# Decoding a candidate's position in a top-k router: sums of comparisons in place of shifts, casts and predicated copies

## The chip, the cores and the metric

The kernel runs on one core of one Trainium2 chip. The metric is the device time of one launch in microseconds (us), lower is better. Three runs of the kernel before gave a median of 3564.58 us (3550.21 to 3570.75).

## The reference

One layer of a hybrid decoder over 1024 tokens of width 1024: a token mixer with three parallel branches (stick-breaking attention, native sparse attention, a gated linear recurrence), merged by sigmoid gates, and then a feed-forward block of experts that are found by product keys. The change lies in that last block, which for a chunk of 128 tokens is

```python
qh = (xc @ w_q).reshape(Ct, 8, 2, 64)
s = jnp.einsum("nhad,akd->nhak", qh, sub_keys)            # 128 sub-keys per half
top_s, top_i = lax.top_k(s, 16)                           # 16 best of each half
cand = (top_s[:, :, 0, :, None] + top_s[:, :, 1, None, :]).reshape(Ct, 8, 256)
cand_idx = (top_i[:, :, 0, :, None] * 128 + top_i[:, :, 1, None, :]).reshape(Ct, 8, 256)
best_s, pos = lax.top_k(cand, 16)
eidx = jnp.take_along_axis(cand_idx, pos, axis=-1)        # one of 16384 experts
gate = jax.nn.softmax(best_s, axis=-1)
hpre = jnp.einsum("nd,nhkd->nhk", xc, u_tab[eidx])
act = gate * gelu(hpre)
y = jnp.einsum("nhk,nhkd->nd", act, v_tab[eidx])
```

So each token has 8 heads and 16 experts per head. From a position in the list of candidates the router has to recover the two ranks, a (in the first half's list) and b (in the second's), and from these the two sub-key numbers.

## The kernel before

**Tiles and parts.** The 1024 tokens are eight tiles of 128 tokens, in four parts of two tiles. The mixer, the merge, the scores and the route of each part are emitted one after the other. The expert block is computed in two ways. For parts 1 and 2 (tiles 2 to 5, 512 tokens) it is dense: a loop over 128 expert groups of 128 experts multiplies all 512 tokens with every expert, and gates that are zero for experts not chosen (kept in DRAM as d_G, loaded as `gt`) do the selection. For parts 0 and 3 (tiles 0, 1, 6 and 7) the rows of u and v are gathered: per tile 128 indirect DMAs for u and 128 for v, issued by GpSimd, each followed by one VectorE update of 128x1024 (`gather_tile`: L1147 for u, L1157 for v into `gacc`). These gathers and updates run beside other work: those of tiles 0 and 1 beside the later parts' mixer, those of tiles 6 and 7 beside the dense loop. Their landing rows cycle through five buffers (eleven for part 3, some of them named `rr_u` and `rr_v`). The tile's index list (`gidx`) has a single buffer and is read by all of its 256 gathers.

**The route of a tile.** `route` (L985) builds for each head 72 candidates instead of 256, since a pair of ranks a and b can be among the 16 best only if (a+1)(b+1) is at most 16. They lie in four blocks: positions 0 to 31 are 2 ranks a by 16 ranks b, 32 to 47 are 2 by 8, 48 to 63 are 4 by 4, 64 to 71 are 8 by 1. The position of a chosen candidate, `p2` (128x128: 8 heads of 16), is decoded to a and b (L1034 to L1048). Then the ranks become one-hot masks of 128x2048 (`oneh`, L1060), which are multiplied with the sub-key numbers (`tir`, put there by ScalarE) and summed by halving (L1064, L1065). For gathered tiles `routes` makes the expert number (L1177), casts it to `idx` (L1178) and stores it; GpSimd's gathers of the tile load it from there. For dense tiles `keep_route` and `spread_pieces` turn ranks and gates into d_G (`hot` on VectorE, `gb` on TensorE).

**Who sets the order.** Two layers. First a plan in Python: pieces of VectorE and TensorE work are emitted by a model of both engines' load; `account` adds up 0.06 us plus elements/960 per VectorE instruction, and a piece is emitted when an engine's load lies below what is due. A route is a generator, and each of its steps up to a `yield` is such a piece; ROUTE_STEPS says how many there are per tile. The pieces of the last part's tail (merge, scores, routes of tiles 6 and 7) go to the list `ending`; those that are left when the dense loop starts are emitted in the loop, TP = 3 behind each expert group. The 1024 gather updates are spread over the plan's steps by `paced`. Then a scheduler orders each engine's instructions by a simulated timeline, so the built order is not the one written.

**The shared ring.** Eight buffers of 128x512 with the tag "at" (`W2` with its defaults) are handed out in turn: to fa, fb and ua of a route (the fields that the decode works in), to its candidate lists and `tir`, to the gelu outputs `ge` of the dense loop and to a copy of a PSUM bank there. A new tenant waits until the one before it in that buffer has been read for the last time.

**The dense loop.** Group i+3's first matmul (`g`, L258) runs ahead of group i's second one (into six PSUM accumulators `acc` and one in SBUF, L1436, L1445). ScalarE makes `ge` from `g` (L1395), VectorE multiplies with `gt` (L1429), and every f32 operand is split into two f16 halves, the high by ScalarE (L213) and the low by VectorE (L214): `us`, `vs` and `ac`.

Of the kernel before, what the change touches and what calls it, by code (L numbers as in the profile page):

```python
# [71 lines left out]
def trunk(ctx: ExitStack, tc: tile.TileContext, a: dict, out: bass.AP):  # L72
# [921 lines left out]
    def route(pt, tile_no, ts_, ti_, gate):  # L994
# [36 lines left out]
        V.tensor_tensor(gate, mb, gz.unsqueeze(2).to_broadcast([128, 8, 16]), op=ALU.mult)  # L1031
        yield

        V.tensor_copy(pf, p2)  # L1034

        V.tensor_scalar(t_u, p2, 4, None, op0=ALU.logical_shift_right)
        V.tensor_copy(af, t_u)
        V.tensor_scalar(t_u, p2, 15, None, op0=ALU.bitwise_and)
        V.tensor_copy(bf, t_u)

        for start, sh, sub, mask in ((32, 3, -2.0, 7), (48, 2, -8.0, 3), (64, 0, -56.0, 0)):
            V.tensor_scalar(t_m, pf, float(start) - 0.5, None, op0=ALU.is_gt)
            V.tensor_scalar(t_u, p2, sh, None, op0=ALU.logical_shift_right)
            V.tensor_scalar(t_f, t_u, sub, None, op0=ALU.add)
            V.copy_predicated(af, t_m, t_f)
            V.tensor_scalar(t_u, p2, mask, None, op0=ALU.bitwise_and)
            V.tensor_copy(t_f, t_u)
            V.copy_predicated(bf, t_m, t_f)  # L1048
            yield

        shape = [128, 16, 16, 8]
        tif = SM(f"tif_{nm}", [128, 8, 2, 16], F16, bufs=1)
# [1 line left out]
        for x, sel in ((0, af), (1, bf)):  # L1054
            tir = W2(f"tir{x}_{nm}", (128, 8, 16, 8), F16)
            S.activation(tir, tif[:, :, x, :].unsqueeze(3).to_broadcast([128, 8, 16, 8]), AF.Copy)
            selh = SM(f"selh{x}_{nm}", [128, 16, 8], F16, bufs=1)
            V.tensor_copy(selh, sel.rearrange("p (g w) -> p g w", w=8))
            oh_ = WT(f"oneh{x}_{nm}", pt, x, shape, F16)
            V.tensor_tensor(oh_, selh.unsqueeze(2).to_broadcast(shape), iota16r.unsqueeze(1).to_broadcast(shape), op=ALU.is_equal)  # L1060
            o4 = oh_.rearrange("p (h u) b w -> p h u (b w)", u=2)
            V.tensor_tensor(o4, o4, tir.rearrange("p h b w -> p h (b w)").unsqueeze(2).to_broadcast([128, 8, 2, 128]), op=ALU.mult)
            for w in (8, 4, 2):
                V.tensor_tensor(oh_[:, :, 0:w, :], oh_[:, :, 0:w, :], oh_[:, :, w:2 * w, :], op=ALU.add)  # L1064
            V.tensor_tensor(sel.rearrange("p (g w) -> p g w", w=8), oh_[:, :, 0, :], oh_[:, :, 1, :], op=ALU.add)  # L1065
            yield
# [97 lines left out]

    found = {}

    ROUTE_STEPS = 11

    def routes(pt, tl, tsa, tia):

# [394 lines left out]
```

## Time and profile before

| what | before |
|---|---|
| median of three runs | 3564.58 us (3550.21 to 3570.75) |
| the profiled execution | 3556.94 us |
| its span | 3555.1 us, mean granted TensorE clock 0.937 |
| TensorE (PE) busy | 3255.7 us, 92% |
| VectorE (DVE) busy | 3001.0 us, 84%, 6662 instructions |
| ScalarE (ACT) busy | 1599.9 us, 45% |
| GpSimd (POOL) busy | 1360.4 us, 38% |
| DRAM traffic | 944.19 MB read, 110.10 MB written, 297 GB/s |

How to read it: one execution is recorded by the hardware profiler. Times are us unless marked ns. L12 is line 12 of the kernel. In a row "out<-in" are the names of the tiles, without their running numbers; fa_rt, fb_rt and ua_rt are the three fields of a route, so the decode's rows carry those names. The bracket at the end of a row of a timeline gives the time that the engine stood idle before the instruction, and what ended it. PE is TensorE, PEld its loading of weights, DVE VectorE, ACT ScalarE, POOL GpSimd. A busy share over the whole span is a mean over stages with different limits. An engine that idles and isn't the limit of a stage costs nothing there.

### The profile page before, as it was taken

How to read it: one execution, taken by the hardware profiler on the slowest of the kernel's cores; microseconds unless marked ns; L12 is line 12 of the kernel's file. 1: busy time of each engine (PE TensorE's matmuls, PEld its weight loads, DVE VectorE, ACT ScalarE, POOL GpSimd, SP SyncE). 2: the span in 40 equal slices, each digit the busy share in tenths (PEclk: the TensorE clock that was granted, in tenths of full speed). 3: DMA queues.
4: the chain of work that ended last, by engine and by line, in shares of the span. 5: the costliest groups of instructions: out<-in, count | busy, mean ns of one | idle time of the engine just before them, and what ended most of it. 6: DMA issues, size and time to landing. Idle time of an engine off the chain costs nothing.

```text
span 3555.1 us, 57087 instructions
## 1 busy us (share of the span) xinstructions
PE 3255.7 (92%) x20660; PEld 2181.6 (61%) x20660; DVE 3001.0 (84%) x6662; ACT 1599.9 (45%) x3162; POOL 1360.4 (38%) x1166
## 2 busy tenths in 40 slices
PE   7999899999997799999878879869999999999996
PEld 6887777777876587887666644434444444444443
DVE  5665669888789888888998868999988998989898
ACT  5776454653543465644356333234334333333332
POOL 0000001343332242223322234347764765766664
PEclk9999999999997799999778899989999999999998
DMA  8964865989977587897656799789998999999997
GB/s 303 322 240 150 279 206 197 327 314 311 360 284 239 170 307 253 307 331 277 219 190 214 278 353 332 242 267 372 388 375 314 375 381 351 371 352 380 342 373 260
DMA packets 359336, 1058.07 MB, mean 298 GB/s; under 512 B 35238, under 2 KB 107626, under 8 KB 354444
## 3 DMA queue, kind: packets, MB, share of 16 engines
q0 software_dynamic: 147456, 536.94, 42.1%
q1 hardware_dynamic: 206988, 483.93, 38.4%
q10 hardware_dynamic: 4608, 33.56, 2.4%
q8 instruction: 162, 2.65, 0.3%
q14 instruction: 122, 1.00, 0.1%
HBM read 944.19 MB, written 110.10 MB: 297 GB/s over the span
## 4 chain that ended last, share of the span: by engine, by line
PE 53%; DVE 23%; DMA 9%; issue 7%; ACT 6%; POOL 1%; SPq 0%; ACTq 0%; DVEq 0%; POOLq 0%
PE g L258 13%; PE acc L1436 10%; PE pj_mg L258 4%; DVE u L1147 4%; PE g L1436 3%; DVE gacc L1157 3%; PE pj_r_hg L258 2%; DMA v<-in_peer_v_dram,gidx 2%; PE pb L258 2%; DMA gt<-d_G 2%; DMA u<-in_peer_u_dram,gidx 2%; PE pj_wo L258 2%; PE gb L1219 1%; PE gb L1220 1%; PE z_sb L410 1%
## 5 line engine op out<-in xcount | busy, mean ns | idle before, releaser
L1155 POOL DMA_INDIRECT v<-in_peer_v_dram,gidx x421 | 553.6, 1315 | 689.8 <-DVE gacc L1157 410.1
L1145 POOL DMA_INDIRECT u<-in_peer_u_dram,gidx x417 | 523.5, 1255 | 636.8 <-DVE u L1147 404.9
L258 PE MATMUL g<-h,us 128*128 128x512 f16 x3072 | 690.8, 382 | 17.1 <-DVE ts L982 6.2
L1157 DVE SCALAR_TENSOR_TENSOR gacc<-v,act,gacc 128x1024 f32<-128x1024 f32 x421 | 538.1, 1278 | 35.4 <-DMA v<-in_peer_v_dram,gidx 31.8
L1436 PE MATMUL acc<-vs,ac 128*128 128x512 f16 x2304 | 536.8, 381 | 20.6 <-ACT vs L213 7.8
L1436 PEld LDWEIGHTS <-ac 128*128 128x128 f16 x3072 | 302.0, 98 | 411.4 <-issue 50.1
L258 PEld LDWEIGHTS <-us 128*128 128x128 f16 x3072 | 302.0, 98 | 385.1 <-issue 17.8
L1147 DVE SCALAR_TENSOR_TENSOR u<-u,gh 128x1024 f32<-128x1024 f32 x417 | 501.8, 1216 | 34.3 <-DMA u<-in_peer_u_dram,gidx 33.8
L1395 ACT ACTIVATE ge<-g 128x512 f32<-128x512 f32 x128 | 76.2, 595 | 528.7 <-PE g L258 498.4
L258 PE MATMUL pj_mg<-hT,w_mg 128*128 128x256 f16 x2304 | 273.9, 274 | 6.3 <-ACT mg L881 3.9
L258 PEld LDWEIGHTS <-w_mg 128*128 128x128 f16 x2304 | 226.8, 100 | 37.6 <-issue 11.8
L1436 PE MATMUL g<-vs,ac 128*128 128x512 f16 x768 | 184.0, 383 | 23.6 <-ACT ge L1395 23.6
L214 DVE SCALAR_TENSOR_TENSOR vs<-vraw,vs 128x1024 f16<-128x1024 f32 x128 | 154.8, 1215 | 25.9 <-ACT vs L213 25.8
L1145 POOL DMA_INDIRECT rr_u<-in_peer_u_dram,gidx x95 | 137.1, 1444 | 89.5 <-DVE rr_u L1147 66.3
L213 ACT ACTIVATE vs<-vraw 128x1024 f16<-128x1024 f32 x128 | 132.6, 1046 | 84.8 <-DMA vraw<-in_peer_v_dram 84.8
L213 ACT ACTIVATE ac<-ge 128x512 f16<-128x512 f32 x128 | 80.0, 628 | 200.7 <-DVE ge L1429 161.3
L1155 POOL DMA_INDIRECT rr_v<-in_peer_v_dram,gidx x90 | 130.7, 1453 | 94.3 <-DVE gacc L1157 71.5
L214 DVE SCALAR_TENSOR_TENSOR us<-uraw,us 128x1024 f16<-128x1024 f32 x128 | 155.6, 1215 | 9.8 <-ACT us L213 9.1
L258 PE MATMUL pb<-o,w_b 128*128 128x256 f16 x1152 | 144.8, 282 | 20.3 <-DVE sg L919 16.7
L1219 PE MATMUL gb<-hot 128*128 128x128 f16 x512 | 126.1, 294 | 39.2 <-DVE hot L1216 21.2
L258 PE MATMUL pj_r_hg<-hT,w_r_hg 128*128 128x256 f16 x1152 | 143.5, 283 | 7.1 <-ACT iv_hg L739 4.7
L1429 DVE TENSOR_TENSOR ge<-ge,gt 128x256 f32<-128x256 f32 x256 | 97.9, 419 | 55.7 <-ACT ge L1395 30.2
(1141 smaller groups left out, 6422.0 us busy)
## 6 DMA issues: line engine op xcount, KB each, us to landing
uraw<-in_peer_uT_dram SPq DMA_DIRECT2D x128, 512.0 KB, 7.2
vraw<-in_peer_v_dram SPq DMA_DIRECT2D x128, 512.0 KB, 8.1
w_mg<-dw SPq DMA_DIRECT2D x72, 512.0 KB, 5.0
gt<-d_G SPq DMA_DIRECT2D x32, 1024.0 KB, 18.5
d_G<-stages ACTq DMA_DIRECT2D x20, 1024.0 KB, 5.2
w_r_hg<-dw SPq DMA_DIRECT2D x36, 512.0 KB, 5.2
w_b<-dw SPq DMA_DIRECT2D x72, 256.0 KB, 5.0
wr_mg<-in_wblk_dram SPq DMA_DIRECT2D x24, 512.0 KB, 4.9
```

What stands on the lines that cost most here:

```text
L213: S.activation(hi, src, AF.Copy, scale=scale)
L214: V.scalar_tensor_tensor(lo, in0=src, scalar=scale, in1=hi, op0=ALU.mult, op1=ALU.subtract)
L258: P.matmul(ps, l[:, k, :], r[:, k, :], start=(i == 0), stop=(i == n - 1))
L410: P.matmul(x["z"], st["q"][b:b + 64, tl * 128:(tl + 1) * 128], st["k"][b:b + 64, r0 + c0:r0 + c1], start=True, stop=(c0 > 0))
L1145: G.indirect_dma_start(out=ur, out_offset=None, in_=a["peer_u"], in_offset=bass.IndirectOffsetOnAxis(ap=idx[:, c:c + 1], axis=0))
L1147: V.scalar_tensor_tensor(ur, in0=ur, scalar=1.0, in1=h2, op0=ALU.mult, op1=ALU.mult, accum_out=hpre[:, c:c + 1])
L1155: G.indirect_dma_start(out=vr, out_offset=None, in_=a["peer_v"], in_offset=bass.IndirectOffsetOnAxis(ap=idx[:, c:c + 1], axis=0))
L1157: V.scalar_tensor_tensor(acc, in0=vr, scalar=act[:, c:c + 1], in1=acc, op0=ALU.mult, op1=ALU.add)
L1219: P.matmul(ps[:, n, :], hs[:, 0, :, n], hs[:, 2, :, n], start=True, stop=False)
L1395: S.activation(ge, ps, AF.Gelu, scale=1.0 / (SW * SH2))
L1429: V.tensor_tensor(gv, gv, gt[:, :, i % 8, :], op=ALU.mult)
L1436: P.matmul(ps, ac[:, x, t * 128:(t + 1) * 128], v[:, y, dh * 512:(dh + 1) * 512], start=start and n == 0, stop=stop and n == 2)
```

## The change

The decode is written anew. Before, af and bf get the values for the first block (shift by 4, mask 15), and then three times, for positions from 32, 48 and 64 on, a mask is made and both ranks are overwritten by predicated copies of the next block's formula: 25 operations and two casts to f16 behind them. Now t is the number of the block, as twice the comparison with 63.5 plus those with 47.5 and 31.5 (so 0, 1, 2 or 4), and 4 - t is the width of the block as a power of two. Rank a is p2 shifted right by that count, less 0, 2, 8 or 56, which two operations make from t as (t(t-1)+2)t. Rank b is p2 less the same shifted value shifted back. Both shifts are by a count that differs per element. The two ranks are written as f16 at once into one tile, `ranks`. The generator yields 10 times instead of 11, so ROUTE_STEPS is 10.

```diff
@@ -1031,22 +1031,22 @@
         V.tensor_tensor(gate, mb, gz.unsqueeze(2).to_broadcast([128, 8, 16]), op=ALU.mult)
         yield
 
+
         V.tensor_copy(pf, p2)
-
-        V.tensor_scalar(t_u, p2, 4, None, op0=ALU.logical_shift_right)
-        V.tensor_copy(af, t_u)
-        V.tensor_scalar(t_u, p2, 15, None, op0=ALU.bitwise_and)
-        V.tensor_copy(bf, t_u)
-
-        for start, sh, sub, mask in ((32, 3, -2.0, 7), (48, 2, -8.0, 3), (64, 0, -56.0, 0)):
-            V.tensor_scalar(t_m, pf, float(start) - 0.5, None, op0=ALU.is_gt)
-            V.tensor_scalar(t_u, p2, sh, None, op0=ALU.logical_shift_right)
-            V.tensor_scalar(t_f, t_u, sub, None, op0=ALU.add)
-            V.copy_predicated(af, t_m, t_f)
-            V.tensor_scalar(t_u, p2, mask, None, op0=ALU.bitwise_and)
-            V.tensor_copy(t_f, t_u)
-            V.copy_predicated(bf, t_m, t_f)
-            yield
+        V.tensor_scalar(t_f, pf, 63.5, 2.0, op0=ALU.is_gt, op1=ALU.mult)
+        V.scalar_tensor_tensor(t_f, in0=pf, scalar=47.5, in1=t_f, op0=ALU.is_gt, op1=ALU.add)
+        V.scalar_tensor_tensor(t_f, in0=pf, scalar=31.5, in1=t_f, op0=ALU.is_gt, op1=ALU.add)
+        V.tensor_scalar(t_m, t_f, -1.0, 4.0, op0=ALU.mult, op1=ALU.add)
+        yield
+        V.tensor_tensor(t_u, p2, t_m, op=ALU.logical_shift_right)
+        V.tensor_tensor(t_m, t_u, t_m, op=ALU.logical_shift_left)
+
+        V.scalar_tensor_tensor(pf, in0=t_f, scalar=-1.0, in1=t_f, op0=ALU.add, op1=ALU.mult)
+        V.scalar_tensor_tensor(pf, in0=pf, scalar=2.0, in1=t_f, op0=ALU.add, op1=ALU.mult)
+        ranks = SM(f"selh_{nm}", [128, 2, 128], F16, bufs=1)
+        V.tensor_tensor(ranks[:, 0], t_u, pf, op=ALU.subtract)
+        V.tensor_tensor(ranks[:, 1], p2, t_m, op=ALU.subtract)
+        yield
 
         shape = [128, 16, 16, 8]
         tif = SM(f"tif_{nm}", [128, 8, 2, 16], F16, bufs=1)
@@ -1054,8 +1054,7 @@
         for x, sel in ((0, af), (1, bf)):
             tir = W2(f"tir{x}_{nm}", (128, 8, 16, 8), F16)
             S.activation(tir, tif[:, :, x, :].unsqueeze(3).to_broadcast([128, 8, 16, 8]), AF.Copy)
-            selh = SM(f"selh{x}_{nm}", [128, 16, 8], F16, bufs=1)
-            V.tensor_copy(selh, sel.rearrange("p (g w) -> p g w", w=8))
+            selh = ranks[:, x].rearrange("p (g w) -> p g w", w=8)
             oh_ = WT(f"oneh{x}_{nm}", pt, x, shape, F16)
             V.tensor_tensor(oh_, selh.unsqueeze(2).to_broadcast(shape), iota16r.unsqueeze(1).to_broadcast(shape), op=ALU.is_equal)
             o4 = oh_.rearrange("p (h u) b w -> p h u (b w)", u=2)
@@ -1164,7 +1163,7 @@
 
     found = {}
 
-    ROUTE_STEPS = 11
+    ROUTE_STEPS = 10
 
     def routes(pt, tl, tsa, tia):
```

The built order changes around it. The first place is VectorE's order in the route of tile 6, which is mixed with the updates of tile 1's gathers (`gacc<-v_N` is the update of row N). fa_rt_24428, fb_rt_24429 and ua_rt_24430 are the fields of tile 6's route before:

```order
L1043 TENSOR_SCALAR ua_rt_24430<-ua_rt_24430 128x128
L1157 SCALAR_TENSOR_TENSOR gacc_33877<-v_110_34209,act_33489,gacc_33877 128x1024
L1042 TENSOR_SCALAR ua_rt_24430<-fa_rt_24428 128x128
L1044 TENSOR_SCALAR fa_rt_24428<-ua_rt_24430 128x128
L1157 SCALAR_TENSOR_TENSOR gacc_33877<-v_111_34212,act_33489,gacc_33877 128x1024
L1045 COPY_PREDICATED fb_rt_24429<-ua_rt_24430,fa_rt_24428 128x128
L1046 TENSOR_SCALAR ua_rt_24430<-ua_rt_24430 128x128
L1157 SCALAR_TENSOR_TENSOR gacc_33877<-v_112_34215,act_33489,gacc_33877 128x1024
L1047 CAST fa_rt_24428<-ua_rt_24430 128x128
L1157 SCALAR_TENSOR_TENSOR gacc_33877<-v_113_34218,act_33489,gacc_33877 128x1024
L1048 COPY_PREDICATED fb_rt_24429<-ua_rt_24430,fa_rt_24428 128x128
L1043 TENSOR_SCALAR ua_rt_24430<-ua_rt_24430 128x128
```

and afterwards its fields are fa_rt_24320 and ua_rt_24322, selh_rt is the tile with the two ranks, and the lines behind the change count one less (L1156 is L1157 of before):

```order
L214 SCALAR_TENSOR_TENSOR us_25065<-uraw_25063,us_25065 128x1024
L1039 TENSOR_SCALAR ua_rt_24322<-fa_rt_24320 128x128
L1044 SCALAR_TENSOR_TENSOR fa_rt_24320<-fa_rt_24320 128x128
L1156 SCALAR_TENSOR_TENSOR gacc_33733<-v_106_34053,act_33345,gacc_33733 128x1024
L1041 TENSOR_TENSOR ua_rt_24322<-ua_rt_24322 128x128
L1045 SCALAR_TENSOR_TENSOR fa_rt_24320<-fa_rt_24320 128x128
L1156 SCALAR_TENSOR_TENSOR gacc_33733<-v_107_34056,act_33345,gacc_33733 128x1024
L1042 TENSOR_TENSOR ua_rt_24322<-ua_rt_24322 128x128
L1047 TENSOR_TENSOR selh_rt_24540<-ua_rt_24322,fa_rt_24320 128x128
L1156 SCALAR_TENSOR_TENSOR gacc_33733<-v_108_34059,act_33345,gacc_33733 128x1024
L1048 TENSOR_TENSOR selh_rt_24540<-ua_rt_24322 128x128
L1059 TENSOR_TENSOR oneh_rt_24607<-selh_rt_24540,iota16r 128x2048
```

Before, the decode's operations stand between updates 109 and 114, with more of the same loop ahead and behind; now the last two ranks are made between updates 106 and 108, and the first one-hot mask follows.

The second place is VectorE's order at the end of the dense loop, where `gacc<-v_N` and `gacc<-rr_v_N` are updates of tile 7, the last gathered one, and the `vs` rows are low halves of v for the loop's last groups:

```order
L214 SCALAR_TENSOR_TENSOR vs_32483<-vraw_32481,vs_32483 128x1024
L1157 SCALAR_TENSOR_TENSOR gacc_35409<-rr_v_115_35736,act_35045,gacc_35409 128x1024 x2
L1157 SCALAR_TENSOR_TENSOR gacc_35409<-rr_v_117_35741,act_35045,gacc_35409 128x1024 x2
L1157 SCALAR_TENSOR_TENSOR gacc_35409<-v_119_35746,act_35045,gacc_35409 128x1024
L1157 SCALAR_TENSOR_TENSOR gacc_35409<-v_120_35749,act_35045,gacc_35409 128x1024
L1157 SCALAR_TENSOR_TENSOR gacc_35409<-v_121_35752,act_35045,gacc_35409 128x1024
L1157 SCALAR_TENSOR_TENSOR gacc_35409<-v_122_35755,act_35045,gacc_35409 128x1024
L1157 SCALAR_TENSOR_TENSOR gacc_35409<-v_123_35758,act_35045,gacc_35409 128x1024
L214 SCALAR_TENSOR_TENSOR vs_32513<-vraw_32511,vs_32513 128x1024
L1157 SCALAR_TENSOR_TENSOR gacc_35409<-v_124_35761,act_35045,gacc_35409 128x1024
L1157 SCALAR_TENSOR_TENSOR gacc_35409<-v_125_35764,act_35045,gacc_35409 128x1024
L214 SCALAR_TENSOR_TENSOR vs_32543<-vraw_32541,vs_32543 128x1024
```

and afterwards:

```order
L214 SCALAR_TENSOR_TENSOR vs_32219<-vraw_32217,vs_32219 128x1024
L1156 SCALAR_TENSOR_TENSOR gacc_35265<-rr_v_126_35623,act_34901,gacc_35265 128x1024 x2
L214 SCALAR_TENSOR_TENSOR vs_32311<-vraw_32309,vs_32311 128x1024
L225 TENSOR_SCALAR gms_fin_35633<-gss_fin_35630 128x1
L214 SCALAR_TENSOR_TENSOR vs_32339<-vraw_32337,vs_32339 128x1024
L1445 TENSOR_TENSOR acc_22949<-acc_22949,p_123_2_32246 128x512
L230 TENSOR_TENSOR gu_fin_35638<-gy_fin_35635 128x1
L1445 TENSOR_TENSOR acc_22949<-acc_22949,p_123_4_32268 128x512
L231 TENSOR_TENSOR gu_fin_35638<-gu_fin_35638,gms_fin_35633 128x1
L232 TENSOR_SCALAR gu_fin_35638<-gu_fin_35638 128x1
L233 TENSOR_TENSOR gy_fin_35635<-gy_fin_35635,gu_fin_35638 128x1
L214 SCALAR_TENSOR_TENSOR vs_32369<-vraw_32367,vs_32369 128x1024
```

Before, ten and more updates of tile 7 stand between the last splits of `vs`; now the last two of them, 126 and 127, stand ahead of those splits, and the small operations of tile 7's final norm (`gms_fin`, `gu_fin`) follow among them.

## The prediction

> **What bounds the kernel now.** I read the page's head and its chain first, for the engines that set the end. Then I read busy time by stretches of the span, to see which engine is full where the changed code runs. Then I read the waits inside the one stretch where TensorE stands still.
>
> ```profile
> span 3555.1 us, 57087 instructions
> PE 3255.7 (92%) x20660; PEld 2181.6 (61%) x20660; DVE 3001.0 (84%) x6662; ACT 1599.9 (45%) x3162; POOL 1360.4 (38%) x1166
> PE 53%; DVE 23%; DMA 9%; issue 7%; ACT 6%; POOL 1%; SPq 0%; ACTq 0%; DVEq 0%; POOLq 0%
> ```
>
> Half of the chain that ended last is TensorE and a quarter VectorE, so neither average decides what a VectorE saving is worth. The stretches below are, in order: the routes of tiles 0 and 1, of 2 and 3, of 4 and 5, of 6 and 7, then the dense expert loop, then the end. Columns are busy us (and instructions) of each engine, the granted clock, the DMA share and GB/s.
>
> ```profile
> 545.00:600.00 55.00, 54.21 (x448) 45.30 (x445) 48.93 (x272) 28.27 (x66) 4.89 (x8) 0.98 0.47 148
> 1085.00:1185.00 100.00, 69.79 (x366) 53.08 (x365) 98.33 (x353) 38.44 (x99) 29.06 (x33) 0.66 0.65 210
> 1700.00:1810.00 110.00, 83.45 (x387) 58.70 (x385) 105.92 (x387) 42.63 (x99) 31.48 (x30) 0.63 0.54 179
> 2250.00:2400.00 150.00, 113.14 (x517) 53.68 (x518) 143.90 (x449) 42.81 (x56) 61.04 (x42) 0.88 0.74 242
> 2400.00:3500.00 1100.00, 1091.28 (x5040) 493.85 (x5039) 1008.15 (x1383) 370.19 (x493) 716.23 (x503) 1.00 0.98 364
> 3500.00:3556.00 56.00, 28.28 (x121) 11.97 (x118) 46.71 (x69) 17.50 (x31) 14.68 (x14) 0.80 0.56 207
> ```
>
> The bound changes by stretch. While tiles 0 and 1 are routed TensorE is full (54.2 of 55 us). While tiles 2 to 5 are routed VectorE is full (98.3 of 100, 105.9 of 110) and TensorE has 30 and 27 us to spare. From 2250 to 2400 VectorE is busy for 143.9 of 150 us and TensorE idles 37. From 2400 to 3500 TensorE idles 9 us of 1100, the DMA engines are at 0.98, and VectorE has 92 us free. At the end TensorE is half idle again.
>
> **The change, part by part.** First the price of the instructions. The rows are by source line; the three figures are minimum, median and maximum ns.
>
> ```profile
> L1036 DVE TENSOR_SCALAR ua_rt<-ua_rt x8: 207/216/261, 561.1 to 2398.2; 128x128 uint32<-128x128 uint32 x8
> L1045 DVE COPY_PREDICATED fb_rt<-ua_rt,fa_rt x24: 275/302/304, 564.3 to 2412.2; 128x128 f32<-128x128 uint32 x24
> L1177 DVE SCALAR_TENSOR_TENSOR fb_rt<-fb_rt x4: 268/279/284, 587.9 to 2480.3; 128x128 f32<-128x128 f32 x4
> L1065 DVE TENSOR_TENSOR fb_rt<-oneh_rt x16: 264/280/291, 585.7 to 2474.8; 128x128 f32<-128x128 f16 x16
> ```
>
> Busy time overstates what an instruction takes from its neighbours, because starts overlap; the timeline of VectorE shows by how much (start us, duration us). The rows are the decode of tile 5, from its first to the first one-hot behind it, and a two-input addition at tile 6.
>
> ```profile
> 1785.85 0.21 DVE L1034 CAST fa_rt<-ua_rt 128x128 f32<-128x128 uint32 x1
> 1785.99 0.21 DVE L1036 TENSOR_SCALAR ua_rt<-ua_rt 128x128 uint32<-128x128 uint32 x1
> ...
> 1787.98 0.30 DVE L1045 COPY_PREDICATED fb_rt<-ua_rt,fa_rt 128x128 f32<-128x128 uint32 x1
> 1788.19 0.22 DVE L1046 TENSOR_SCALAR ua_rt<-ua_rt 128x128 uint32<-128x128 uint32 x1
> 1788.45 0.23 DVE L1047 CAST fa_rt<-ua_rt 128x128 f32<-128x128 uint32 x1
> ...
> 1791.52 1.22 DVE L1060 TENSOR_TENSOR oneh_rt<-selh_rt,iota16r 128x2048 f16<-128x2048 f16 x1
> 2329.29 0.28 DVE L1011 TENSOR_TENSOR cand_rt<-ts 128x128 f32<-128x128 f32 x1
> 2329.49 0.19 DVE L1030 RECIPROCAL gz_rt<-gz_rt 128x8 f32<-128x8 f32 x1
> ```
>
> A one-input instruction takes 0.14 us from start to start when the next one doesn't read it (1785.85 to 1785.99), and its 0.22 us plus 0.04 when the next one does (1788.19 to 1788.45). A two-input one takes 0.20 to 0.21 free (2329.29 to 2329.49), and by the same 0.04 some 0.32 when read at once. Per tile 27 instructions go: 21 with one input (4 at L1036 to L1039, 15 in the loop, 2 casts at L1058) and 6 predicated copies. Ten come: 2 with one input and 8 with two (4 like L1177, 4 like L1065; two of the latter shift by a per-element count, which no row shows, and I bound them by 0.20 and 0.32 too). Net 17 per tile, 136 in 8 tiles. The old decode of tile 5 took 5.67 us (1785.85 to 1791.52); some 0.65 of it was other work between its rows, so 5.0. The new one takes 0.14 for the kept cast plus 2 x 0.14 + 8 x 0.20 = 2.0 us if no neighbour reads the one before, and 0.14 + 2 x 0.26 + 8 x 0.32 = 3.2 us if all do. The saving is 1.8 to 3.0 us a tile. About half of the new chain stands directly behind its producer in the built order, so I take the middle, 2.3.
>
> Tiles 2 to 5: VectorE is the full engine, so 4 x 2.3 = 9.2 us off the path (7.2 to 12.0). Tiles 0 and 1: TensorE's 54.2 us of 55 cover it; I take 0, and 2 x 2.3 = 4.6 if that cover is gone. The emission plan pulls some projection pieces one step forward, and is the same again before the dense loop; I cost that at nothing, since the same matmuls fill the same stretches.
>
> Tile 6 is worth more than its instructions, because of what waits for it. The rows are TensorE's, then ScalarE's, then VectorE's and GpSimd's timelines.
>
> ```profile
> 2332.41 2.75 PE L1436 MATMUL g<-vs,ac 128*128 128x512 f16 x12
> ...
> 2361.99 4.87 PE L1436 MATMUL g<-vs,ac 128*128 128x512 f16 x12 [22.94 <-ACT ge L1395]
> 2361.34 0.60 ACT L1395 ACTIVATE ge<-g 128x512 f32<-128x512 f32 x1 [27.67 <-DVE fb_rt L1048]
> 2341.01 1.28 DVE L1157 SCALAR_TENSOR_TENSOR gacc<-v,act,gacc 128x1024 f32<-128x1024 f32 x1
> 2361.01 0.29 DVE L1048 COPY_PREDICATED fb_rt<-ua_rt,fa_rt 128x128 f32<-128x128 uint32 x1
> 2390.61 1.88 POOL L1155 DMA_INDIRECT v<-in_peer_v_dram,gidx  x1 [1.46 <-DVE oneh_rt L1064]
> 2402.41 0.97 POOL L1145 DMA_INDIRECT u<-in_peer_u_dram,gidx  x1 [9.92 <-DVE ua_rt L1043]
> ```
>
> The gelu output of expert group 18 needs a slot of the ring that fa, fb, ua, tir and ge share, and it gets one when the last predicated copy of tile 6 has run. ScalarE stood 27.67 us for that, and TensorE 22.94, because its PSUM bank was not read. The decode was long there since the scheduler had put a gather row's update between nearly every two of its instructions: 16 of them (rows 102 to 117 of tile 1) between L1026 and that copy. In the changed order group 18 takes another slot, released by the first one-hot product, and only rows 102 to 109 stand ahead of it. Row 109 is the update at 2341.01. Behind it stand 1.2 us of its own and three one-hot operations of some 1.1 us start to start; so the slot comes at 2341.0 + 1.2 + 3.4 = 2345.6 instead of 2361.3, 15.7 us earlier. Late next is the copy of the following PSUM bank, which now waits for the second one-hot product, behind rows 110 to 113; that is 4 rows and half a one-hot reduction, some 10 us later, or 2355.6 against 2362.4 and after. Between 7 and 15.7 us are gained; I take 11. Bounds: 0 if VectorE's other work between the same rows is what TensorE needs, and 25 = 22.94 + 2.12 if the wait goes wholly.
>
> The 2.12 us are 4.87 - 2.75: the twelve matmuls behind the wait were slower than the twelve ahead of it. The Trainium skill (TensorE: Matmul & The Clock Gate, Part 1) says that TensorE's clock falls to half after an idle window of about 3.4 us, whatever the wait's length beyond it, and needs as long to recover. By that rule a wait cut from 22.9 to about 12 us pays the slow matmuls again, and the sum stays without the 2.12; by the row alone, taking the slowness in proportion, about 1 us more would be gained.
>
> The index of tile 6 is also stored earlier: it stands before the update of row 120 of tile 1, not of row 127. GpSimd waited 9.92 us for it at 2402.41. This moves the whole stream of 512 gathers of tiles 6 and 7 ahead of the matmuls: 8 updates more stand before expert group 32, and 22 more before group 112. I cost this at nothing from 2400 to 3500, where TensorE is full and VectorE's 92 free us cover 22 x 1.28 = 28 us. It pays at the end. The first two rows are VectorE's, the third TensorE's, the last two the groups from 3505 to 3540.
>
> ```profile
> 3518.66 6.57 DVE L1157 SCALAR_TENSOR_TENSOR gacc<-v,act,gacc 128x1024 f32<-128x1024 f32 x5
> 3529.93 2.60 DVE L1157 SCALAR_TENSOR_TENSOR gacc<-rr_v,act,gacc 128x1024 f32<-128x1024 f32 x2
> 3526.41 4.63 PE L1436 MATMUL acc<-vs,ac 128*128 128x512 f16 x12 [6.67 <-DVE vs L214]
> L1436 PE MATMUL acc<-vs,ac 128*128 128x512 f16 x72 | 19.2, 410 | 8.8 <-DVE vs L214 7.2 <-ACT vs L213 1.6
> L1157 DVE SCALAR_TENSOR_TENSOR gacc<-v,act,gacc 128x1024 f32<-128x1024 f32 x11 | 14.1, 1283 | 0.3
> ```
>
> TensorE's last matmuls wait 8.8 us for the last splits of v, which stand behind gather updates on VectorE. In the changed order two updates are left there. The wait is worth 0 to 8.8 us; I take 6, since the splits also need their loads.
>
> Sum: 9.2 + 0 + 11 + 6 = 26.2 us. The profiled execution took 3556.94 us (its span and 1.8 us around it), so 3530.7 against it. It lies 7.6 us under the median of the three runs, 3564.58, so against the median 3538.4.
>
> **The rivals.** (B) The dense loop gives the ending back: the DMA engines stand at 0.98 there, and if they set its pace, TensorE starts sooner and waits later. For it speaks that share; against it that TensorE idles 9 us in 1100. Only tiles 2 to 5 are left, 9 us: 3555, between 3549 and 3560. (C) The shortened decode doesn't shorten the path, because VectorE waits for gathered rows where it used to decode. For it speaks the wait of updates for landings:
>
> ```profile
> L1157 DVE SCALAR_TENSOR_TENSOR gacc<-v,act,gacc 128x1024 f32<-128x1024 f32 x421 | 538.1, 1278 | 35.4 <-DMA v<-in_peer_v_dram,gidx 31.8
> ```
>
> Against it: 31.8 us in 421 updates is little, and from 1085 to 1185 VectorE idles 1.7 us. That gives 3565, with 6 us either way. (D) Slower: updates that now stand ahead of the same matmuls block VectorE, because their rows haven't landed. Rows come at (3529.9 - 2402.4) / 510 = 2.2 us apiece; 22 updates that VectorE reaches before their rows cost 22 x 2.2 = 48 us, of which 9.2 + 11 are paid for: +28, or 3593. It decides from the point at which these waits exceed some 20 us between 2400 and 3500. Against it: the stream itself starts earlier, by up to the 9.92 us of GpSimd's wait, and has the TensorE stall's time to run ahead.
>
> **How the numbers follow.** The forecast (A) has 0.56: 3538, with a range of its own from 3526 (12 + 15.7 + 8.8 = 36.5, and about 2 of tiles 0 and 1) to 3551 (7.2 + 4 + 2). B has 0.20, C 0.11 and D 0.13. What a measurement of this kernel tells from no change is about 0.5%, 17.8 us: faster is below 3546.8, slower above 3582.4. Faster: 0.50 of A and 0.02 of B. Same: 0.06 of A, 0.18 of B, C, and 0.03 of D; slower: 0.10. The range from 3520 to 3575 leaves out most of D and the edge of A towards the bound of 25 us at tile 6.
>
> **What would show it.** VectorE has 136 instructions less, and the ten new ones of a tile last 0.21 to 0.30 us each. From 1085 to 1185 and from 1700 to 1810 the same work ends some 4 to 5 us sooner apiece. ScalarE's longest wait for a ring slot falls from 27.7 to about 12 us, and TensorE's with it. GpSimd's wait between tiles 1 and 6 is under 5 us. The last update of tile 7 comes before the last split of v. I am wrong if TensorE's idle time from 2400 to 3500 grows beyond 25 us, if a wait of over 10 us appears at tile 7's route, or if the dense loop starts no earlier than now.

## The result and the profile after

The changed kernel is slower: 3587.8 us (median of 7 runs, 3574.53 to 3595.68) against 3561.23 us (7 runs, 3550.21 to 3570.75), a ratio of 1.0075 with a 95% interval of 1.0058 to 1.0092. A second series gave 1.0082 (1.0065 to 1.0100). The forecast was 3538 us, between 3520 and 3575. Two single executions further on, of 5116.82 us and 13694.03 us, lie far from all others of their kernels, and no ratio counts them. The page of the profiled execution (3585.7 us):

```profile
span 3583.9 us, 56939 instructions
PE 3268.6 (91%) x20660; PEld 2183.7 (61%) x20660; DVE 2984.4 (83%) x6526; ACT 1604.2 (45%) x3167; POOL 1343.1 (37%) x1166
```

VectorE (DVE) has exactly the 136 instructions less (6662 to 6526), and 16.6 us less busy time. The span is 28.8 us longer all the same. By stretches, with the columns of before:

```profile
2250.00:2400.00 150.00, 108.98 (x496) 50.67 (x495) 146.35 (x437) 46.78 (x60) 56.76 (x45) 0.88 0.76 250
2400.00:3500.00 1100.00, 1059.01 (x4833) 475.51 (x4832) 982.18 (x1321) 350.13 (x466) 703.57 (x498) 0.98 0.97 358
3500.00:3590.00 90.00, 70.61 (x328) 31.77 (x325) 60.91 (x89) 33.18 (x51) 16.23 (x15) 0.94 0.45 166
```

From 2400 to 3500 TensorE idles 41 us where it idled 9. Three points of ScalarE's timeline divide the span: the gelu of group 20, the gelu of the last group, 127, and the end. Before:

```profile
2398.49 0.60 ACT L1395 ACTIVATE ge<-g 128x512 f32<-128x512 f32 x1
...
2400.87 0.59 ACT L1395 ACTIVATE ge<-g 128x512 f32<-128x512 f32 x1
2401.35 1.06 ACT L223 ACTIVATE sqf<-gacc 128x1024 f32<-128x1024 f32 x1
...
3505.23 0.60 ACT L1395 ACTIVATE ge<-g 128x512 f32<-128x512 f32 x1 [5.45 <-PE g L258]
```

After, from the gelu of group 18 on:

```profile
2340.54 0.60 ACT L1394 ACTIVATE ge<-g 128x512 f32<-128x512 f32 x1 [12.44 <-DVE oneh_rt L1061]
...
2391.77 1.06 ACT L223 ACTIVATE sqf<-gacc 128x1024 f32<-128x1024 f32 x1 [12.14 <-DVE gacc L1156]
...
2398.68 1.08 ACT L1394 ACTIVATE ge<-g 128x512 f32<-128x512 f32 x2
...
3552.74 0.60 ACT L1394 ACTIVATE ge<-g 128x512 f32<-128x512 f32 x1 [2.67 <-PE g L258]
```

Group 18's wait for its ring slot is 12.44 us instead of 27.67, as forecast. But group 20 runs at 2398.7, where it ran at 2398.5: the gain is gone two groups later. From there to the last group the changed kernel loses 47.3 us. From the last gelu to the end it takes 31.2 us instead of 49.9, so 18.7 come back: 0.2 + 47.3 - 18.7 = 28.8.

Where the gain of tile 6 went, TensorE's timeline shows:

```profile
2341.19 4.90 PE L1435 MATMUL g<-vs,ac 128*128 128x512 f16 x12 [6.67 <-ACT ge L1394]
2349.02 7.00 PE L258 MATMUL g<-h,us 128*128 128x512 f16 x24 [2.93 <-ACT p L1444]
...
2399.33 7.44 PE L258 MATMUL g<-h,us 128*128 128x512 f16 x24 [21.30 <-ACT ge L1394]
```

The waits were 22.94 and 5.08 us; now they are 6.67, 2.93 and 21.30. ScalarE's queue is in order. Before, `sqf`, the square for tile 1's final norm, stood behind the gelus of groups 20 and 21 (2401.35). In the changed order it stands ahead of them, and it waits 12.14 us for tile 1's last update; from its start at 2391.77 to the gelu of group 20 another 6.9 us go by.

What TensorE waited for from 2402 to 3505, in us, times and longest; before:

```profile
PE acc L1436 <- ACT vs L213: 6.2, 2, 4.4
PE g L258 <- ACT p L1445: 2.5, 1, 2.5
```

and after:

```profile
PE acc L1435 <- ACT vs L213: 21.3, 7, 5.5
PE acc L1435 <- DVE vs L214: 7.9, 8, 3.3
PE g L258 <- ACT p L1444: 7.3, 2, 5.1
PE g L1435 <- ACT ge L1394: 4.3, 4, 2.4
```

All are operands that come through VectorE or ScalarE: the split of v, the copy of a PSUM bank, the gelu. The gather stream of tiles 6 and 7 meanwhile kept its own time. Its last issue on GpSimd (POOL) before, and its first and last after:

```profile
3518.42 1.01 POOL L1155 DMA_INDIRECT rr_v<-in_peer_v_dram,gidx  x1 [0.30 <-issue]
```

```profile
2393.10 1.20 POOL L1144 DMA_INDIRECT rr_u<-in_peer_u_dram,gidx  x1 [7.27 <-DMA gidx<-d_idx]
...
3522.65 1.02 POOL L1154 DMA_INDIRECT rr_v<-in_peer_v_dram,gidx  x1 [0.30 <-issue]
```

That is 2.18 us a row before (from 2402.41) and 2.21 after. A reading that the experiments test: the rows come no faster, and more of them stand ahead of the late groups on VectorE (20 more at group 112, 23 at group 124), so 44 to 51 us of lateness at 2.2 us each.

### The profile page after: what moved, and what is told of

The parts are those of the page before. It is cut to its first block, busy times and chain, and to the rows that moved or that the text cites. A ratio compares the mean times of both kernels' runs of the same rounds, so it can differ in the third digit from the quotient of the medians.

```text
span 3583.9 us, 56939 instructions
## 1 busy us (share of the span) xinstructions
PE 3268.6 (91%) x20660; PEld 2183.7 (61%) x20660; DVE 2984.4 (83%) x6526; ACT 1604.2 (45%) x3167; POOL 1343.1 (37%) x1166
## 5 line engine op out<-in xcount | busy, mean ns | idle before, releaser
L1154 POOL DMA_INDIRECT v<-in_peer_v_dram,gidx x421 | 540.4, 1284 | 720.9 <-DVE gacc L1156 437.1
L1144 POOL DMA_INDIRECT u<-in_peer_u_dram,gidx x417 | 534.1, 1281 | 630.4 <-DVE u L1146 395.0
L258 PE MATMUL g<-h,us 128*128 128x512 f16 x3072 | 697.0, 384 | 43.3 <-ACT ge L1394 21.5
L1435 PE MATMUL acc<-vs,ac 128*128 128x512 f16 x2304 | 543.4, 384 | 33.5 <-ACT vs L213 21.3
L1156 DVE SCALAR_TENSOR_TENSOR gacc<-v,act,gacc 128x1024 f32<-128x1024 f32 x421 | 538.0, 1278 | 23.1 <-DMA v<-in_peer_v_dram,gidx 19.8
L258 PE MATMUL pb<-o,w_b 128*128 128x256 f16 x1152 | 145.5, 284 | 14.5 <-DVE sg L919 11.6
L1154 POOL DMA_INDIRECT rr_v<-in_peer_v_dram,gidx x90 | 119.4, 1326 | 97.6 <-DVE gacc L1156 79.0
```

Source lines behind the costliest of these rows:

```text
L258: P.matmul(ps, l[:, k, :], r[:, k, :], start=(i == 0), stop=(i == n - 1))
L1144: G.indirect_dma_start(out=ur, out_offset=None, in_=a["peer_u"], in_offset=bass.IndirectOffsetOnAxis(ap=idx[:, c:c + 1], axis=0))
L1154: G.indirect_dma_start(out=vr, out_offset=None, in_=a["peer_v"], in_offset=bass.IndirectOffsetOnAxis(ap=idx[:, c:c + 1], axis=0))
L1156: V.scalar_tensor_tensor(acc, in0=vr, scalar=act[:, c:c + 1], in1=acc, op0=ALU.mult, op1=ALU.add)
L1435: P.matmul(ps, ac[:, x, t * 128:(t + 1) * 128], v[:, y, dh * 512:(dh + 1) * 512], start=start and n == 0, stop=stop and n == 2)
```

## The experiments

Ratios are to the kernel before, run beside them, with 95% intervals. "Updates ahead of group 112" counts, in VectorE's built order, the gather updates ahead of that group's split of `ac`: 936 before, 956 after. Times are medians; a profile shows one execution, which can lie 10 us off its kernel's median (new_67: 3582.0 against 3573.5, new_norm22: 3572.1 against 3582.1).

**Which tiles' decode does it.** Two kernels hold both decodes:

```diff
+        new = tile_no < 6          # new_67: tile_no >= 6
+        if new:
             ...the new decode, 10 steps
+        else:
             ...the old decode, 11 steps
```

> New decode in tiles 0 to 5, the old one in tiles 6 and 7; from the dense loop on, VectorE's built order has as many gather updates ahead of each expert group as before (936 ahead of group 112). Theory 1 (the slowdown comes from VectorE's order in the dense loop, which the decode of tiles 6 and 7 changes): 3557 us, 4 us under before, since the loop's first gelu was 4.3 us earlier in the changed kernel. Theory 2 (it comes from what the decode of tiles 6 and 7 does to the waits at the loop's 18th to 20th group, whatever stands behind): 3557 too. Theory 3 (the plan of the first tiles is what costs): 3585 us.

Measured: 3563.46 us, 1.0019 (1.0003 to 1.0036).

> Old decode in tiles 0 to 5, the new one in tiles 6 and 7; 955 updates ahead of group 112, as in the changed kernel (956). Theories 1 and 2: 3591 us, the changed kernel's 3587.8 and the 4 us that the first tiles no longer save. Theory 3: 3563 us.

Measured: 3573.46 us, 1.0032 (1.0016 to 1.0048); last gelu at 3548.5 us in the profile. The plan of the first tiles is not the main cause, since with the new decode there alone the time is within 5 us of before. But the numbers miss: the first tiles save nothing, and the decode of tiles 6 and 7 alone costs 15 us, not 27 to 30. The two parts alone sum to some 20 us.

**The order against the decode.** The first kernel queues the n-th update of tiles 6 and 7 behind the group k that stood ahead of it before. The second has the old decode, and queues each group's split behind about the number of updates that the changed order has there.

```diff
+        pts = ((19, 0), (24, 20), (32, 56), ..., (112, 424), (124, 477), (127, 497), (128, 512))
+        return tc.issue_after(gmark[min(held(n), NI - 1)])     # new_held; gmark[k]: split of ac, group k
```

```diff
+    ahead = ((20, 5), (24, 27), (32, 63), ..., (112, 444), (120, 483), (124, 500), (127, 512))
+            tc.add_manual_dep(gmark[k], upds[n - 1].name, ...)  # old_ahead; n: 512 + the interpolated number - 15
```

> New decode everywhere, but each update of tiles 6 and 7 is queued on VectorE behind the expert group that stood ahead of it before (933 updates ahead of group 112 instead of 956). Theory 1: the dense loop no longer falls behind: 3552 us (3545 to 3560), TensorE idle under 15 us from 2400 to 3500. Theory 2: the waits at groups 18 to 20 are unchanged and so is the time: 3585 us.

Measured: 3557.39 us, 1.0001 (0.9987 to 1.0014).

> Old decode everywhere, but from group 20 on the low split of ac of each group is queued on VectorE behind as many gather updates as in the changed kernel (956 ahead of group 112 instead of 936). Theory 1: the old kernel becomes as slow as the changed one: 3588 us (3578 to 3598), with the last gelu some 45 us later than the 3505 of before and a tail that is 19 us shorter. Theory 2: 3561 us, as before.

Measured: 3572.45 us, 1.0039 (1.0023 to 1.0055). The rows from 2400 to 3500, of new_held and then of old_ahead:

```profile
2400.00:3500.00 1100.00, 1096.12 (x5078) 496.59 (x5076) 996.65 (x1341) 365.99 (x488) 718.43 (x496) 1.00 0.99 362
```

```profile
2400.00:3500.00 1100.00, 1060.89 (x4887) 478.88 (x4885) 1008.84 (x1353) 355.88 (x473) 711.25 (x507) 0.98 0.99 365
```

TensorE idles 4 us in the first and 39 in the second. So the order decides: the new decode in the old order loses nothing, and the old decode with updates moved ahead loses 14 us. new_held's last gelu is at 3496.1 us and old_ahead's at 3534.1. Still, old_ahead reaches half of the changed kernel's loss, and new_held gains nothing on before.

old_ahead is not the changed order in its detail. It has the same 956 updates ahead of group 112, but its lead over before jumps to 19 at group 31 and is mostly 13 to 18 up to group 96, where the changed order's is mostly 5 to 9. The jump is one wait of TensorE:

```profile
2502.11 4.99 PE L1444 MATMUL acc<-vs,ac 128*128 128x512 f16 x12 [23.29 <-DVE ac L214]
```

Counted from the gelu of group 20, that of group 32 comes 24.9 us later than before, that of group 112 still only 23.1, and the last 37.3 (the changed kernel: 7.0, 35.4 and 47.3). So this run shows that updates put ahead of a group hold TensorE up. It does not show that the changed order costs the same with the old decode.

**The same kernel again**, for the series that follow.

> The changed kernel once more, as the yardstick of the three beside it: 3588 us, 1.0075 of before. A second profile of it should show the same as the first: 20th gelu at about 2398 us, last gelu 45 us or so later than before's 3505, and a tail some 19 us shorter.

Measured: 3584.34 us, 1.0082; last gelu at 3552.3 us, TensorE's wait at group 20 21.5 us.

**The wait at group 20.** The final norm of tile 1 goes behind the gelu of group 22 on ScalarE.

```diff
-        y = rms_scale(acc, f"fin{ti}", rows(f"sqf{ti}"), "g")
+        with tc.issue_after(gel[22]) if ti == 1 else ExitStack():
+            y = rms_scale(acc, f"fin{ti}", rows(f"sqf{ti}"), "g")
```

> The changed kernel with the final norm of tile 1 queued on ScalarE behind the gelu of group 22 instead of ahead of that of group 20. Both theories: TensorE's wait of 21.3 us for the gelu of group 20 is shorter, by up to the 12.1 us that ScalarE waited for tile 1's last update. Theory 1 (the order of VectorE in the loop and the full DMA engines set the end; 949 updates stand ahead of group 112): what is won there is given back in the loop, 3585 us (3578 to 3592). Theory 2 (the waits at groups 18 to 20 set the end): 3576 us, all 12 us are kept.

Measured: 3582.07 us, 1.0085 (1.0063 to 1.0107). ScalarE's and TensorE's rows:

```profile
2379.39 1.08 ACT L1397 ACTIVATE ge<-g 128x512 f32<-128x512 f32 x2
...
3536.23 0.60 ACT L1397 ACTIVATE ge<-g 128x512 f32<-128x512 f32 x1 [1.84 <-PE g L258]
```

```profile
2380.04 6.85 PE L258 MATMUL g<-h,us 128*128 128x512 f16 x24 [3.27 <-ACT ge L1397]
...
2397.55 4.75 PE L1439 MATMUL acc<-vs,ac 128*128 128x512 f16 x10 [8.07 <-ACT ac L213]
```

Group 20 runs 19 us earlier and TensorE's wait of 21.3 us is 3.3, with another of 8.1 behind it. The median is that of the changed kernel (3584.3 us), so theory 1 fits. But the profiled execution, the fastest of six, took 3572.1 us, and its last gelu came 16.5 us earlier than the changed kernel's; the interval of the ratio reaches down to some 3576 us, theory 2's time. Whether an earlier loop is kept in the changed order is therefore not settled here.

**Fewer updates ahead than before.** `return 20 + n * 10 // 43`, 903 ahead of group 112.

> New decode, gather updates held further back than before: 4.3 a group from group 20 on, 903 ahead of group 112 (before 936) and 969 ahead of group 127 (before 1009). Theory 1: TensorE doesn't wait in the loop, and can't go faster than before, so the last gelu stays at about 3495; 55 updates are left behind the last group, at 1.3 to 1.4 us each: 3495 + 75 + 12 us of ending, 3580 us (3570 to 3592). Rival (the fewer updates ahead, the better, since what they block is TensorE alone): 3545 us.

Measured: 1.0118 (1.0097 to 1.0140), 3601.39 us (3598.7 without the execution of 5116.82 us; the profile is of that one, and isn't read). Both theories miss. Holding back too far costs as much as standing too far ahead, or more.

**Both fixes together**, the held order and the norm behind group 22.

> New decode, gather updates held to their old places (932 ahead of group 112), and the final norm of tile 1 queued on ScalarE behind the gelu of group 22, so that TensorE's wait of 21.2 us at group 20 shrinks to about 11. Theory 1a (the loop is paced by VectorE's order and TensorE together; the DMA engines' load is not the limit): the loop runs as in the kernel with held updates alone, from a start that is 15 to 19 us earlier, and keeps it: 3540 us (3533 to 3547). Theory 1b (the gather stream has its own pace of 2.2 us a row, set by the DMA engines): the stream ends when it did, at about 3524 us, and the time is 3555 us.

Measured: 3569.78 us, 1.0033 (1.0016 to 1.0049): both theories miss. In the profile group 20 runs at 2387.3 us, but the last gather is issued at 3537.3 us instead of new_held's 3524.0. Of these 13 us some 7 are there when the stream starts (2397.6 against 2390.7), behind a loop that began 8 us later (2095.4 against 2087.3), and the rest is its pace (2.23 against 2.22 us a row). The time follows the stream's end, as in theory 1b: both kernels end 25 to 30 us behind the last issue. Why the pace differs I didn't settle.

**What the loop runs out of.** Four kernels relieve one resource each. Half of each group's u load (the half is used twice):

```diff
+        load(raw[:, 0:4], a["peer_uT"][i][:, 0:4])
```

> The changed kernel, with half of each expert group's u loaded (256 KB less per group; the half that is there is used twice), and the gather updates held to about the changed kernel's places (947 ahead of group 112, 1021 ahead of group 127). Theory 1 (the DMA engines are the limit, so updates that stand further ahead push the matmuls back): with 128 x 0.26 MB = 33.5 MB less to move, some 90 us at 374 GB/s, TensorE hardly idles from 2400 to 3500 (under 12 us instead of 41), the last gelu is at about 3500 and the time about 3535 us. Rival (updates ahead of the splits cost VectorE's time, or wait for the latency of a gather, and the DMA's load doesn't matter): 3588 us, TensorE idle about 40 us.

Measured: 3563.63 us, 1.0022 (1.0009 to 1.0035), between the two. No wait of TensorE for a split of v is left from 2402 to 3505, but 38 us for gelus and PSUM copies are. From the gelu of group 20 to the last one the loop takes 24.6 us more than before. The last gather is issued at 3522.3 us, as in the changed kernel.

The loads of gt on another queue, `nc.scalar.dma_start(gt, ...)`:

> The changed kernel with the loads of gt (two of 1 MB each per eight expert groups) issued on ScalarE's queue instead of SyncE's; VectorE's built order is the same, row by row. Theory Q (TensorE's waits for the split of v come from the v loads that stand in SyncE's queue behind a u load, which itself is held for 10 to 13 us behind the two gt loads): the 18 to 21 us of these waits go, TensorE idles some 20 us from 2400 to 3500 instead of 41, and the time is 3565 us. Rival (the loads are late because the DMA engines are full, whichever queue issues them): 3584 us, with the same waits. If ScalarE is held by the issue as SyncE was, it shows as idle time ahead of the rows behind each gt load on ScalarE, and the run says nothing on either.

Measured: 3605.58 us, 1.0135 (1.0108 to 1.0162). ScalarE is held by the issue, up to 13 us for one load and 18.4 us for the first pair (from 2089.6), and group 20 already runs 19 us later than in the changed kernel. So this run decides nothing, as its expectation said:

```profile
2870.06 10.39 ACTq L1423 DMA_DIRECT2D gt<-d_G  x1
2880.50 1.06 ACT L213 ACTIVATE vs<-vraw 128x1024 f16<-128x1024 f32 x1 [9.83 <-issue]
```

In the changed kernel the same holds SyncE (SP) behind the two gt loads; the v loads then go out late, and ScalarE's split of v waits. The first row is of the kernel before, which has such a hold too; it is not what the change brought:

```profile
3086.67 10.89 SPq L100 DMA_DIRECT2D uraw<-in_peer_uT_dram  x1
```

```profile
3103.36 3.64 SPq L1423 DMA_DIRECT2D gt<-d_G  x2
3107.05 12.21 SPq L100 DMA_DIRECT2D uraw<-in_peer_uT_dram  x1
3119.37 1.17 SPq L100 DMA_DIRECT2D vraw<-in_peer_v_dram  x2
```

```profile
3135.32 1.06 ACT L213 ACTIVATE vs<-vraw 128x1024 f16<-128x1024 f32 x1 [6.69 <-DMA vraw<-in_peer_v_dram]
```

Then half of each update's work on VectorE, and half of each gathered row (the update reads it twice); both hold the updates to the changed kernel's places:

```diff
+                w = 512 if ti >= 6 else D                       # half_update
+                V.scalar_tensor_tensor(acc[:, 0:w], in0=vr[:, 0:w], ...)
```

```diff
+                G.indirect_dma_start(out=vr[:, 0:512], ..., in_=a["peer_v"].rearrange("r (a c) -> (r a) c", a=2), ...)   # half_rows
```

> The changed kernel with the gather updates held to about the changed kernel's places (947 ahead of group 112, 1024 ahead of group 127), and each update of tiles 6 and 7 on VectorE over 512 of the 1024 columns; gathers and loads are whole. In all kernels so far the gathers of tiles 6 and 7 came at 2.17 to 2.23 us a row. Theory V (VectorE, at 0.9 busy and in order, sets that pace): the update falls from 1.28 to about 0.68 us, the pace under 2.12 us, so that TensorE at 10.3 us a group is the limit: last gelu near 3505 us, time 3540 us (3530 to 3550). Theory D (the transfers) and theory G (GpSimd's issue, 1.44 us busy a gather): pace 2.2 us and 3584 us as in the changed kernel.

Measured: 3550.68 us, 0.9981 (0.9958 to 1.0004), at a pace of 2.14 us a row: near theory V, just outside its range.

> The same holding (947 and 1021), and each gather of tiles 6 and 7 brings 512 columns instead of 1024, that is 134 MB less from 2400 us on, a third of what is moved there; the update reads them twice, so it has 1024 columns to work on and its old time. Theory D: the pace falls under 2.12 us a row and the time to 3540 us (3530 to 3550). Theory V: 2.2 us a row and 3584 us, save the waits for late v loads (18 to 21 us), 3565 us. Theory G: the same, unless GpSimd's busy time a gather falls from 1.44 us, which would show in its rows.

Measured: 3539.99 us, 0.9961 (0.9946 to 0.9976), at 2.12 us a row: theory D's time. The windows of half_update and of half_rows:

```profile
2400.00:3500.00 1100.00, 1083.43 (x5006) 490.16 (x5006) 761.69 (x1361) 365.30 (x487) 584.04 (x514) 1.00 0.99 369
```

```profile
2400.00:3500.00 1100.00, 1090.56 (x5037) 493.48 (x5037) 1019.57 (x1368) 371.19 (x494) 765.18 (x514) 0.99 0.75 249
```

With half rows the DMA engines are at 0.75, and VectorE, at 1019.6 of 1100 us fuller than in any run with whole rows, keeps TensorE fed in the changed order: from 2402 to 3505 TensorE waits once for a gelu (19.9 us, the wait at group 20) and 3 us for splits. So the transfers are one thing that the order runs out of. With half updates the DMA engines stay at 0.99 and the late loads return in part (6.6 us for splits of v), but VectorE has the room to make them up. Either resource alone, relieved, takes the loss away. My reading is that it needs both: loads that come late because the DMA engines are full, and an engine in order that has no slack behind them. GpSimd's issue (theory G) is out by half_rows alone, where a gather costs it 1.49 us (765.18 us, 514 instructions) and the pace fell all the same; with half updates that cost fell to 1.14.

One control is missing: no run has these places, 9 updates nearer to before at group 112 than the changed order, with loads, rows and updates all whole. The run with half of u has them (947 and 1021) and still loses 24.6 us in the loop, so the places alone don't take the loss away; how much of it they take is not known.

**Is an earlier loop kept there?** The old decode in the loop of half_rows, beside half_rows once more on the same chip:

> The old decode in all tiles, in the loop of the run with half rows: each gather of tiles 6 and 7 brings 512 of 1024 columns, and the updates are held to the changed kernel's places (947 updates ahead of group 112). Beside half_rows (new decode, the same loop, 3540 us) it shows what the decode is worth where the loop runs at TensorE's pace. If an earlier start of the loop is kept there (theory S): the old decode starts the loop 4 us later, and its waits at groups 18 to 20 sum to 28 us against 30 to 31, so 3542 us (3540 to 3546). If the new decode's waits at tile 7 outweigh it: 3536 us.

> The run with half rows and the new decode once more, on the same chip as the old decode beside it: 3540 us.

Measured: 3537.09 us, 0.9946 (0.9932 to 0.9961) with the old decode; 3542.6 us, 0.9962 (0.9948 to 0.9976) with the new. TensorE's waits, old decode first:

```profile
2359.86 4.36 PE L1470 MATMUL g<-vs,ac 128*128 128x512 f16 x12 [21.90 <-ACT ge L1428]
2397.00 7.14 PE L258 MATMUL g<-h,us 128*128 128x512 f16 x24 [5.59 <-ACT ge L1428]
```

```profile
2348.98 4.23 PE L1469 MATMUL g<-vs,ac 128*128 128x512 f16 x12 [7.37 <-ACT ge L1427]
2356.81 8.01 PE L258 MATMUL g<-h,us 128*128 128x512 f16 x24 [3.61 <-ACT p L1478]
2407.55 8.23 PE L258 MATMUL g<-h,us 128*128 128x512 f16 x24 [20.72 <-ACT ge L1427]
```

They sum to 27.5 us with the old decode and 31.7 with the new. So even where the loop runs at TensorE's pace the new decode brings no gain; the 5.5 us between the medians go the other way, with intervals that overlap. The old decode's time is near the second forecast, but not for its reason: from the loop's first gelu to its last the two profiles take 1408.9 and 1408.4 us, and the difference is there at the first (2091.0 against 2097.4 us).

## Why the prediction was wrong, point by point

**The prices held.** The eight new two-input operations of a tile last 0.26 to 0.29 us each (the shift by a per-element count 0.28), and some 0.20 us from start to start in tile 1 (L1041 at 578.70, L1045 at 578.90, L1042 at 579.11). 136 instructions are gone. The forecast of 0.20 to 0.32 us from start to start was right.

**Tiles 2 to 5: the saving was there, and didn't reach the end.** Between two fixed points of VectorE's order, the subtraction of the best score (L1026) of tile 2 and the first `hot`, all four kernels with the old decode in the first tiles took 76.8 us, and the eleven profiled with the new one there 70.0 to 70.9. For tile 4 the stretch is 68.1 to 68.2 against 58.9 to 60.6. That is 6.3 + 8.2 = 14.5 us. Not all of it is the decode: the order shifted, and in the two profiles 2.2 us of VectorE's other work have left the first stretch and 2.7 the second. About 10 us remain, near the 9.2 forecast. But the first gelu of the loop came at 2091.1 us on the mean of the four and at 2092.0 on the mean of the eleven. The first of the two stretches and the one behind it, before:

```profile
1113.70:1190.50 76.80, 50.35 (x171) 35.78 (x172) 73.26 (x253) 33.61 (x85) 17.23 (x25) 0.53 0.50 153
1190.50:1727.70 537.20, 507.73 (x3962) 423.69 (x3961) 458.22 (x1147) 292.18 (x631) 173.09 (x161) 0.96 0.81 285
```

and after:

```profile
1117.10:1187.40 70.30, 45.56 (x164) 31.27 (x164) 66.13 (x214) 31.66 (x82) 19.78 (x25) 0.57 0.54 168
1187.40:1728.90 541.50, 510.08 (x3971) 425.86 (x3971) 460.46 (x1153) 293.20 (x634) 168.85 (x161) 0.95 0.81 283
```

On the means of the four and the eleven, 8.6 us are lost ahead of tile 2's point, 4.3 between the two stretches and 2.4 behind the second.

Most of the 8.6 us fits a step that the prediction put at nothing: "the emission plan pulls some projection pieces one step forward [...]; I cost that at nothing, since the same matmuls fill the same stretches". Between the points of tiles 0 and 1 TensorE runs 188 matmuls in all eleven profiles and 147 in all four; the extra ones are nearly all projections. Behind tile 1's point they are missing. In the 24.5 us from there TensorE idles 7.9 to 8.8 us in the eleven and 2.0 in the four, and its granted clock falls. Before, then after:

```profile
577.90:602.40 24.50, 22.53 (x178) 18.07 (x177) 19.90 (x65) 17.16 (x30) 6.31 (x7) 0.98 0.58 173
```

```profile
575.50:600.00 24.50, 16.64 (x70) 9.65 (x68) 20.37 (x55) 14.78 (x27) 10.50 (x11) 0.68 0.82 286
```

For the 4.3 us, TensorE's cover is a reading from one profile of each: the shorter stretch covers 4.8 us less of TensorE's work, and the next one, where TensorE is nearly full, is 4.3 us longer. So "VectorE is the full engine" did not make its whole saving "off the path". That the sum is nil is from all fifteen profiles, in which the loop's start varies by 10 us; the 4 us that new_0to5's expectation counted on lie within that.

**Tile 6: the first wait as forecast, the next one not.** The slot came at 2340.5 us (forecast 2345.6), and the PSUM copy behind it cost 2.93 us. The step that failed is "late next": I named that copy, and not what follows in ScalarE's order, where `sqf` had moved ahead of group 20. The waits sum to 30.9 us instead of 28.0, so the 11 us are -3. The matmuls behind a wait stayed slow: 4.90 us for twelve after 6.67 us of wait, against 2.75. The Trainium skill (TensorE: Matmul & The Clock Gate, Part 1) puts the fall of the clock at an idle window of about 3.4 us, whatever lies beyond it; the trace agrees, as the wait was 22.94 us before and the twelve took 4.87. But the 24 behind the 2.93 us wait took 7.00 us against 5.34, though that wait is under the window. The granted clock (the third number from the end) stood at 1.00 during that wait and fell to 0.51 behind it, so here the measurement decides, and 2.93 us were enough:

```profile
2346.10:2349.00 2.90, 0.00 (x0) 0.00 (x0) 2.90 (x9) 0.60 (x1) 2.60 (x2) 1.00 0.81 270
2349.00:2352.50 3.50, 3.48 (x9) 1.25 (x9) 3.50 (x9) 2.04 (x3) 1.51 (x2) 0.51 0.83 256
```

**The dense loop: D's price, without D's wait.** "I cost this at nothing from 2400 to 3500, where TensorE is full and VectorE's 92 free us cover 22 x 1.28 = 28 us" is the step that decided. The 92 us were not free. They are waits of an engine in order. From group 20 to the last the changed kernel lost 47.3 us (44.7 in its second profile), where the forecast had 0. By the rows: at group 112, with 20 more updates ahead (the prediction counted 22), 35.4 and 32.4 us; at group 124, with 23, 44.5 and 41.9. That is 1.6 to 1.9 us a row, between the 1.28 us of an update and the 2.2 of a gathered row. The price isn't fixed: in old_ahead the same 20 cost 23.1 us at group 112, 1.2 each.

Rival D, with a chance of 0.13, had 48 us for 22 rows and 3593 us. That its price came so near is in part luck, for its mechanism did not show. D was to decide once VectorE's waits for rows that haven't landed exceed 20 us between 2400 and 3500; they were 2.6 us. Its argument against (the stream starts earlier) is true by 9 us, and the stream was no earlier at the end. What grew are VectorE's waits for late v loads. Before, then after (us, times, longest):

```profile
DVE vs L214 <- ACT vs L213: 24.4, 10, 8.0
```

```profile
DVE vs L214 <- ACT vs L213: 50.0, 12, 11.8
...
DVE u L1146 <- DMA u<-in_peer_u_dram,gidx: 2.6, 5, 0.7
```

These waits are not the whole cause either: old_ahead loses 37.3 us in the loop with 19.8 us of them, less than before.

**The end: the sign held, the size didn't.** The ending is 18.7 us shorter, not 6, since all updates stand ahead of the last splits. But it is the other half of the same move: what no longer waits at the end has pushed the loop back.

**What stays open.** The changed kernel loses 27 to 30 us. Updates moved ahead, with the old decode, lose 14, and the decode of tiles 6 and 7 alone, in nearly the changed order, 15. That the first tiles' decode adds the rest was not isolated: alone it costs 5 us (1.0019). By which path a lead in VectorE's order holds TensorE up (late v loads, full DMA engines, VectorE itself) is argued from the half runs, not isolated.

## What to carry to other kernels

Where two streams share one in-order engine and the DMA engines are full, the interleaving is the schedule: count how many items of one stream stand ahead of the other's before and after, and price each at about its busy time at the least and the pace of its transfers at the most (here 1.28 and 2.2 us; 1.2 to 1.9 were measured), not at nothing. A saving on that engine lets a scheduler that plans by its busy time pull one stream forward, so pin the interleaving before judging such an edit. Where work is pulled forward, look for the hole that it leaves behind. And take a stage's saving to the end only after asking which engine is full in the next stage, and what work the shorter stage no longer hides.

## What the runs showed of the hardware that I had not expected

The issue of a load is not always short: behind two gt loads one u load held SyncE's queue for 12.21 us (the median of these loads is 0.33 us), and a gt load held ScalarE for 10.39 us, with what stands behind it. A DMA share near 1.0 was no sign of the bytes alone: with half of u loaded it stayed at 0.95 while the rate fell from 358 to 337 GB/s, and only half rows brought it to 0.75. The run with half of u:

```profile
2400.00:3500.00 1100.00, 1069.26 (x4915) 482.59 (x4915) 991.27 (x1336) 356.03 (x477) 716.41 (x498) 0.99 0.95 337
```

And TensorE's granted clock was 0.51 behind a wait of only 2.93 us, as shown above.
